# First expert table transposed by VectorE in 32x32 blocks, loaded by column quarters, in place of TensorE transposes

## The chip, the core and the metric

The kernel runs on one core of one Trainium2 chip. The metric is device time in microseconds of that core; lower is better. Five engines work beside each other, each in the order of its own queue: TensorE (PE in the rows; its weight loads are PEld), VectorE (DVE), ScalarE (ACT), GpSimd (POOL) and SyncE (SP), which here issues most of the transfers.

## What is computed

One transformer block on 512 tokens of 2048 features: an mLSTM and an S5 mixer, an output projection, and then an expert layer (PEER). The expert layer is what the change touches:

```python
def peer(x, wq, subkeys, u_tab, v_tab):
    q = (x @ wq)...                       # 512 x 2048 by 2048 x 2048
    ...                                   # top-16 of two sub-key scores, softmax gate
    def block(args):
        xt, it, gt = args
        ue = jnp.take(u_tab, it, axis=0)
        ve = jnp.take(v_tab, it, axis=0)
        act = jax.nn.gelu(jnp.einsum('td,ted->te', xt, ue))
        return jnp.einsum('te,ted->td', gt * act, ve)
```

`u_tab` (the first expert table) and `v_tab` (the second) hold 16384 experts of 2048 features in fp32, 128 MB each. `x` is the second RMS norm of the block, with the gain `norm2_g`.

## The kernel before

Of the 512 tokens, the first 128 (`NG`) take their experts by gathers (`gsteps`, L1080): for each of 128 picks of a token one indirect transfer from POOL brings 2048 features per token, and one VectorE pass of 2048 columns multiplies and sums (L1088 for the first table, L1095 for the second). The other 384 tokens (`ND`) go densely: all 16384 experts are read in 128 tiles of 128 experts, and for each tile the activations of all 384 tokens are computed.

A dense product wants the contracted dimension on the partitions. For the first table that is the feature, so a tile of 128 experts x 2048 features must be transposed. `u_load` (L1039) fetches a tile with one transfer of 1 MB, expert by partition, into `ur` (two buffers). `u_unit(i, q)` (L1049) takes a quarter, four blocks of 128 features: four TensorE transposes into one PSUM bank (L1054), then `split` (L88 to L90): ScalarE rounds the bank to `uh`, and VectorE subtracts to get the rest `ul`. `h_unit(i, q)` (L1062) is twelve matmuls of 384 columns (`mm3`, L92 to L95, three per feature block), and after the fourth quarter ScalarE applies the gelu to `hg` (L1071). `h_step` (L1103) keeps `u_unit` two quarters ahead of `h_unit`; `uh` and `ul` have four buffers each.

The order of work on every engine is that in which the Python code emits it (`manual_schedule`). What is called a unit below is one `h_step`: on VectorE the `ul` subtraction, then whatever the step pulls in from the side lists. Three stretches follow one another:

- From 1034 us: the rest of the routing of the tokens (`route_head`, `route_end`), one piece per unit.
- Then `gbuild` (L1112): for 384 tokens, four at a time, VectorE makes eight 128x128 selection matrices (L1122, L1123), TensorE multiplies four pairs, ScalarE copies the product to `Gb`. That is 96 units with such work. After each 128 tokens eight transfers issued by ScalarE write `Gb` out (L1132). In every fourth unit one gather step runs, except while these writes go out. This loop (L1140) covers 44 tiles; it ends at about 1596 us.
- From 1596 us to 3148 us the other 84 tiles (L1214). Here two units alternate with one `v_unit` (L1195) of the second table, 24 matmuls of 384 columns, from the fifth tile on. On VectorE the order of such a pair is: `ul`, `ul`, per tile a `w_stage` (L1164: product, ScalarE rounding, subtraction), one or two gather steps, the subtraction `vl` (1024 columns), two additions into `accT` (L1207).

Then the second table is finished alone (3148 to 3585 us). Ahead of all this, `load_w` (L123) loads the weights of the projections in chunks of 512 KB, 32 of them from `wq`; `norm_k` (L170) transposes the normed tokens `xs` into `xh` and `xl`, which are used by the `wq` projection and, as copies `xdh` and `xdl`, by `h_unit`.

Of the kernel before, what the change touches and what calls it, by code (L numbers as in the profile page):

```python
# [8 lines left out]
F32 = mybir.dt.float32  # L9
F32R = mybir.dt.float32r  # L10
I32 = mybir.dt.int32
U32 = mybir.dt.uint32
AF = mybir.ActivationFunctionType
OP = mybir.AluOpType
# [4 lines left out]
P = 128  # L19
T = 512  # L20
D = 2048
KB = D // P
# [8 lines left out]
def dap(ap, offset, dims):  # L31
    return bass.AP(tensor=ap.tensor, offset=ap.offset + offset, ap=dims)
# [3 lines left out]
def hybrid_block(ctx: ExitStack, tc: tile.TileContext, x, norm1_g, w_in, b_gates, conv_w, mnorm_g,  # L36
# [3 lines left out]
    v, s, g, pe, sp = nc.vector, nc.scalar, nc.gpsimd, nc.tensor, nc.sync  # L40
# [9 lines left out]

    x2 = x[0]
    win = w_in[0]
    out2 = out[0]

    consts = ctx.enter_context(tc.tile_pool(name="consts", bufs=1))
# [9 lines left out]
    def tp_bank(shape=(P, 512), dtype=F32):  # L65
        return ps.tile(list(shape), dtype, name="tp", bufs=4)
# [6 lines left out]
    with pool(name="tmp", bufs=1, side="right") as tmp:  # L73
        iota_i = tmp.tile([P, P], I32, name="iota_i")
        g.iota(iota_i, pattern=[[1, P]], base=0, channel_multiplier=-1)
        v.tensor_scalar(ident, iota_i, 0.0, None, op0=OP.is_equal)

        cst = tmp.tile([96, P], F32, name="cst")
        sp.dma_start(cst[0:64], conv_w[0].rearrange("k (c p) -> (k c) p", p=P))
        sp.dma_start(cst[64:80], norm1_g[0].rearrange("(k p) -> k p", p=P))  # L80
        sp.dma_start(cst[80:96], norm2_g[0].rearrange("(k p) -> k p", p=P))
        p = tp_bank([P, 96])
        pe.transpose(p, cst, ident[:96, :96])
        v.tensor_copy(cvec, p)
# [3 lines left out]
    def split(hi, lo, src):  # L88
        s.activation(hi, src, AF.Copy)  # L89
        v.tensor_tensor(lo, src, hi.bitcast(F32), op=OP.subtract)  # L90
# [32 lines left out]
    def load_w(src, k0, c0):  # L123
        n = NW if src is win and c0 == base["v"] else 256
        raw = wtile("wr", F32, n)
        row = src.ap[0][0]
        cut = lambda c, n: dap(src, k0 * P * row + c, [[row, P], [P * row, 4], [1, n]])
        sp.dma_start(raw[:, :, :256], cut(c0, 256))
        if n > 256:
            sp.dma_start(raw[:, :, 256:], cut(4096, 8))  # L130
        return raw
# [6 lines left out]
    OORDER = (2, 3, 0, 1)  # L138
    chunks = [(win, 4 * q, base[a] + 256 * i) for a, i in plan for q in (OORDER if (a, i) == plan[-1] else range(4))]
    chunks += [(w_out[0], 4 * q, 256 * c) for c in range(8) for q in OORDER]  # L140
    chunks += [(wq[0], 4 * q, 256 * c) for c in range(8) for q in range(4)]
    W = {"raw": [], "ready": [], "n": 0, "p": 0}

    def w_fetch():
# [25 lines left out]
    def norm_k(src, gc, k):  # L170
        p = tp_bank([P, TB, P])
        for tb in range(TB):
            pe.transpose(p[:, tb, :], src[tb][:, k * P:(k + 1) * P], ident)  # L173
        pf = p.rearrange("p b t -> p (b t)")
        s.activation(xh[:, k, :], pf, AF.Copy, scale=gc[:, k:k + 1])
        v.scalar_tensor_tensor(xl[:, k, :], pf, gc[:, k:k + 1], xh[:, k, :].bitcast(F32),
                               op0=OP.mult, op1=OP.subtract)

    XQ = {"n": 16, "f": None}

# [12 lines left out]
    for tb in range(TB):  # L193
# [3 lines left out]
        r = rstd(n1, ss, 1, 1.0 / D, "r1")  # L197
# [681 lines left out]
    with pool(name="n2", bufs=1) as n2:  # L879
        xs = [n2.tile([P, D], F32, name=f"xs{tb}") for tb in range(TB)]  # L880
        ss = n2.tile([P, TB], F32, name="ss2")
        v.tensor_reduce(ss, ssq, axis=AX.X, op=OP.add)
        r = rstd(n2, ss, TB, 1.0 / D, "r2")
        for tb in range(TB):
            if tb < 2:
                v.tensor_scalar(xs[tb], h1[:, tb, :], r[:, tb:tb + 1], None, op0=OP.mult)
            else:
                s.activation(xs[tb], h1[:, tb, :], AF.Copy, scale=r[:, tb:tb + 1])
        for k in range(KB):
            norm_k(xs, g2c, k)  # L890
        g2 = n2.tile([P, D], F32, name="g2")
        bcast_row(g2, norm2_g, D)
        for b in range(NB):
            v.tensor_tensor(xG[b], xs[b], g2, op=OP.mult)
        sk = n2.tile([P, 2, P], F32, name="sk")
        sp.dma_start(sk, subkeys[0].rearrange("a k d -> k a d"))
        p = tp_bank([P, 2, P])
        for a in range(2):
            pe.transpose(p[:, a, :], sk[:, a, :], ident)
        v.tensor_copy(subT, p)  # L900
        g.iota(iotaF, pattern=[[1, P]], base=0, channel_multiplier=0, allow_small_or_imprecise_dtypes=True)
# [136 lines left out]

    def u_load(i):  # L1039
        ur = up.tile([P, D], F32, name="ur", bufs=2)  # L1040
        sp.dma_start(ur, u2[i * P:(i + 1) * P, :])
        UT["r", i] = ur

    u_load(0)
# [2 lines left out]
    accG = [up.tile([P, D], F32, name=f"accG{i}") for i in range(NB)]  # L1047

    def u_unit(i, q):  # L1049
        ur = UT["r", i]  # L1050
        p = tp_bank([P, 4, P])
        for a in range(4):
            k = q * 4 + a
            pe.transpose(p[:, a, :], ur[:, k * P:(k + 1) * P], ident)  # L1054
        uh = up.tile([P, 4, P], F32R, name="uh", bufs=4)
        ul = up.tile([P, 4, P], F32R, name="ul", bufs=4)
        split(uh, ul, p)
        UT["u", i, q] = (uh, ul)
        if q == 3 and i + 2 < NTL:
            u_load(i + 2)  # L1060
# [282 lines left out]
```

## Time and profile before

| | us |
|---|---|
| median of 3 runs | 3587.71 (3583.08 to 3588.83) |
| span of the profiled execution | 3585.1 |
| of it: before the first unit | 1034 |
| units with routing and `gbuild` (44 tiles) | 562 |
| units beside the second table (84 tiles) | 1552 |
| second table alone, end | 437 |

The span runs from the first to the last instruction of one profiled execution; it is 2.6 us less than the median. Over the whole span TensorE is busy for 97%, VectorE for 68%, ScalarE for 34%. A group row gives busy time and mean duration of one instruction, and behind the second bar the idle time of the engine right before it and what ended that. Successive instructions of VectorE overlap a little in the rows: the next one starts before the duration of the last is over.

### The profile page before, as it was taken

What the parts mean: (1) busy time and instruction counts of PE and PEld (TensorE: products, weight loads), DVE (VectorE), ACT (ScalarE), POOL (GpSimd) and SP (SyncE); (2) the same over time, 40 slices, a digit from 0 to 9 for tenths busy, and PEclk for the clock granted to TensorE, in tenths of its full rate; (3) what the DMA queues carried; (4) which work ended last, traced back from release to release, by engine and by line L of the source; (5) the groups of instructions that cost most, each with busy time, mean ns of one, the idle gap of its engine ahead of it and who ended that gap; (6) DMA issues with size and microseconds to landing.
All of it is one profiled execution on the core that took longest, in us unless ns stands there. A gap on an engine that the chain in (4) does not pass through costs nothing.

```text
span 3585.1 us, 53549 instructions
## 1 busy us (share of the span) xinstructions
PE 3473.1 (97%) x21436; PEld 3326.9 (93%) x21436; DVE 2434.8 (68%) x4689; ACT 1208.4 (34%) x1854; POOL 464.8 (13%) x403
## 2 busy tenths in 40 slices
PE   7999999999999999999999999999999999999998
PEld 6888888997889999999999999999999999999997
DVE  7567444325998776846777777777777777766666
ACT  5344554325233333323322222222222222222333
POOL 2001110000000000002222222222222222200000
PEclk9999999999999999999999999999999999999999
DMA  4423443542324567487777767777777777664553
GB/s 143 111 80 103 110 112 105 166 132 84 95 101 159 192 218 233 167 304 269 271 283 279 275 261 268 282 282 277 267 276 274 279 281 266 261 234 169 176 178 119
DMA packets 309706, 729.86 MB, mean 204 GB/s; under 512 B 28240, under 2 KB 183888, under 8 KB 258896
## 3 DMA queue, kind: packets, MB, share of 16 engines
q1 hardware_dynamic: 215824, 411.92, 33.4%
q0 software_dynamic: 44096, 289.34, 22.0%
q10 hardware_dynamic: 49536, 25.17, 2.3%
q8 instruction: 169, 2.77, 0.3%
q14 instruction: 81, 0.66, 0.1%
HBM read 673.40 MB, written 50.59 MB: 202 GB/s over the span
## 4 chain that ended last, share of the span: by engine, by line
issue 38%; PE 35%; DMA 10%; DVE 8%; POOL 6%; ACT 2%; POOLq 0%; ACTq 0%; SPq 0%; DVEq 0%
PE mm L95 11%; PE mm L94 11%; PE mm L93 11%; DMA gr<-in_peer_v_dram,gidx 9%; POOL gr L1076 5%; DVE accG L1095 2%; DVE ul L90 1%; PE tp L1054 1%; POOL Tt L691 1%; DVE vl L90 1%; DVE wl L90 1%; DMA gr<-in_peer_u_dram,gidx 0%; PE tp L173 0%; PE tp L1003 0%; DVE accT L1207 0%
## 5 line engine op out<-in xcount | busy, mean ns | idle before, releaser
L93 PE MATMUL mm<-xdh,uh 128*128 128x384 f32 x2048 | 734.9, 359 | 12.5 <-ACT uh L89 12.5
L95 PE MATMUL mm<-ewh,vl 128*128 128x384 f32 x2048 | 692.8, 338 | 27.0 <-DVE vl L90 27.0
L95 PE MATMUL mm<-xdh,ul 128*128 128x384 f32 x2048 | 693.1, 338 | 3.1 <-DVE ul L90 1.7
L93 PE MATMUL mm<-ewh,vh 128*128 128x384 f32 x2048 | 690.8, 337 | 5.0 <-ACT vh L89 5.0
L94 PE MATMUL mm<-xdl,uh 128*128 128x384 f32 x2048 | 690.7, 337 | 0.0
L94 PE MATMUL mm<-ewl,vh 128*128 128x384 f32 x2048 | 689.6, 337 | 0.0
L89 ACT ACTIVATE uh<-tp 128x512 fp32r<-128x512 f32 x512 | 305.4, 597 | 993.5 <-PE tp L1054 948.4
L90 DVE TENSOR_TENSOR ul<-tp,uh 128x512 fp32r<-128x512 f32 x512 | 343.0, 684 | 255.5 <-ACT uh L89 255.4
L95 PEld LDWEIGHTS mm<-ewh,vl 128*128 128x128 f32 x2048 | 387.5, 189 | 34.2 <-DVE vl L90 34.0
L93 PEld LDWEIGHTS mm<-xdh,uh 128*128 128x128 f32 x2048 | 387.5, 189 | 14.4 <-ACT uh L89 14.1
L95 PEld LDWEIGHTS mm<-xdh,ul 128*128 128x128 f32 x2048 | 386.4, 189 | 7.8 <-DVE ul L90 7.8
L93 PEld LDWEIGHTS mm<-ewh,vh 128*128 128x128 f32 x2048 | 387.6, 189 | 5.3 <-ACT vh L89 5.3
L94 PEld LDWEIGHTS mm<-xdl,uh 128*128 128x128 f32 x2048 | 388.7, 190 | 0.0
L94 PEld LDWEIGHTS mm<-ewl,vh 128*128 128x128 f32 x2048 | 387.5, 189 | 0.0
L1095 DVE SCALAR_TENSOR_TENSOR accG<-gr,acts,accG 128x2048 f32<-128x2048 f32 x127 | 298.1, 2347 | 96.4 <-DMA gr<-in_peer_v_dram,gidx 95.7
L90 DVE TENSOR_TENSOR wl<-wr,wh 128x1024 fp32r<-128x1024 f32 (+1 forms) x144 | 187.1, 1302 | 249.5 <-ACT wh L89 249.4
L1088 DVE SCALAR_TENSOR_TENSOR gr<-gr,xG 128x2048 f32<-128x2048 f32 x128 | 292.1, 2286 | 79.3 <-DMA gr<-in_peer_u_dram,gidx 79.3
L90 DVE TENSOR_TENSOR vl<-vr,vh 128x1024 fp32r<-128x1024 f32 x256 | 312.5, 1221 | 43.8 <-ACT vh L89 43.7
L1076 POOL DMA_INDIRECT gr<-in_peer_u_dram,gidx x128 | 177.6, 1387 | 1262.7 <-DVE gr L1088 957.8
L1207 DVE TENSOR_TENSOR accT<-mm,accT 128x384 f32<-128x384 f32 x496 | 257.4, 549 | 84.1 <-PE mm L95 84.1
L1054 PE MATMUL tp<-ident,ur 128*128 128x128 f32 x2048 | 306.7, 272 | 0.3 <-DMA ur<-in_peer_u_dram 0.3
L93 PE MATMUL mm<-wh,xh 128*128 128x256 f32 (+1 forms) x1024 | 295.3, 288 | 0.0
(393 smaller groups left out, 5315.1 us busy)
## 6 DMA issues: line engine op xcount, KB each, us to landing
ur<-in_peer_u_dram SPq DMA_DIRECT2D x128, 1024.0 KB, 6.2
vr<-in_peer_v_dram SPq DMA_DIRECT2D x128, 1024.0 KB, 5.0
wr<-in_w_in_dram SPq DMA_DIRECT2D x80, 512.0 KB, 3.7
gt_d<-Gb ACTq DMA_DIRECT2D x24, 1024.0 KB, 12.1
gt<-gt_d SPq DMA_DIRECT2D x128, 192.0 KB, 7.6
wr<-in_w_out_dram SPq DMA_DIRECT2D x32, 512.0 KB, 3.6
wr<-in_peer_wq_dram SPq DMA_DIRECT2D x32, 512.0 KB, 3.5
hg_d<-hg SPq DMA_DIRECT2D x44, 192.0 KB, 2.6
```

Source lines behind the costliest of these rows:

```text
L89: s.activation(hi, src, AF.Copy)
L90: v.tensor_tensor(lo, src, hi.bitcast(F32), op=OP.subtract)
L93: pe.matmul(o, ah, bh, start=start, stop=False)
L94: pe.matmul(o, ah, bl, start=False, stop=False)
L95: pe.matmul(o, al, bh, start=False, stop=stop)
L691: g.dma_start(Tt[b % 2][j * 16:(j + 1) * 16, :, j:, :], Ks[:, :, 0:8 - j, :])
L1054: pe.transpose(p[:, a, :], ur[:, k * P:(k + 1) * P], ident)
L1076: g.indirect_dma_start(out=t, out_offset=None, in_=tab, in_offset=bass.IndirectOffsetOnAxis(ap=gidx[:, b, j:j + 1], axis=0))
L1088: v.scalar_tensor_tensor(t, t, 1.0, xG[b], op0=OP.mult, op1=OP.mult, accum_out=acts[:, b, j:j + 1])
L1095: v.scalar_tensor_tensor(accG[b], t, acts[:, b, j:j + 1], accG[b], op0=OP.mult, op1=OP.add)
L1207: v.tensor_tensor(a, o, a, op=OP.add)
```

## The change

Transposing moves from TensorE to VectorE, which transposes 32x32 blocks inside each group of 32 partitions. For the blocks to come out right, a tile of the first table is loaded by column quarters: partitions 32q to 32q+31 hold column quarter q of the tile, four groups of 32 experts side by side. One VectorE instruction over 128 x 512 then gives a `ut` in SBUF with 128 features on the partitions. Which features stand together changes (a block k now holds columns 32k to 32k+31 of each quarter), so the norm gain, the normed tokens and the rows of `wq` are put in the same order. `uh` and `ul` go from four buffers to three, and `ut` has two.

```diff
+    wqt = wq[0]
...
-        sp.dma_start(cst[80:96], norm2_g[0].rearrange("(k p) -> k p", p=P))
+        sp.dma_start(cst[80:96].rearrange("k (q d) -> k q d", q=4),
+                     norm2_g[0].rearrange("(q k d) -> k q d", q=4, k=KB))
...
+        if src is wqt:
+            for q in range(4):
+                sp.dma_start(raw[q * 32:q * 32 + 32],
+                             dap(src, (q * 512 + k0 * 32) * row + c0, [[row, 32], [32 * row, 4], [1, 256]]))
+            return raw
...
+    def quads(t):
+        return t.rearrange("t (k q d) -> t q k d", k=KB, q=4)
...
         for tb in range(TB):
+            o, i = quads(xs[tb]), h1[:, tb, :].rearrange("t (q k d) -> t q k d", q=4, k=KB)
             if tb < 2:
-                v.tensor_scalar(xs[tb], h1[:, tb, :], r[:, tb:tb + 1], None, op0=OP.mult)
+                v.tensor_scalar(o, i, r[:, tb:tb + 1], None, op0=OP.mult)
             else:
-                s.activation(xs[tb], h1[:, tb, :], AF.Copy, scale=r[:, tb:tb + 1])
+                s.activation(o, i, AF.Copy, scale=r[:, tb:tb + 1])
...
-            v.tensor_tensor(xG[b], xs[b], g2, op=OP.mult)
+            fv = lambda t: t.rearrange("t (q k d) -> t q k d", q=4, k=KB)
+            v.tensor_tensor(fv(xG[b]), quads(xs[b]), fv(g2), op=OP.mult)
...
     def u_load(i):
         ur = up.tile([P, D], F32, name="ur", bufs=2)
-        sp.dma_start(ur, u2[i * P:(i + 1) * P, :])
+        for q in range(4):
+            sp.dma_start(ur[q * 32:q * 32 + 32].rearrange("p (e c) -> p e c", e=4),
+                         dap(u2, i * P * D + q * 512, [[D, 32], [32 * D, 4], [1, 512]]))
...
     def u_unit(i, q):
-        ur = UT["r", i]
-        p = tp_bank([P, 4, P])
-        for a in range(4):
-            k = q * 4 + a
-            pe.transpose(p[:, a, :], ur[:, k * P:(k + 1) * P], ident)
-        uh = up.tile([P, 4, P], F32R, name="uh", bufs=4)
-        ul = up.tile([P, 4, P], F32R, name="ul", bufs=4)
-        split(uh, ul, p)
+        ut = up.tile([P, 4, P], F32, name="ut", bufs=2)
+        uh = up.tile([P, 4, P], F32R, name="uh", bufs=3)
+        ul = up.tile([P, 4, P], F32R, name="ul", bufs=3)
+        uq = UT["r", i].rearrange("p (e k d) -> p k e d", e=4, k=KB)
+        v.transpose(ut.rearrange("p k (e d) -> p k e d", e=4), uq[:, q * 4:q * 4 + 4])
+        split(uh, ul, ut)
         UT["u", i, q] = (uh, ul)
```

## Rows read from the trace of the kernel before

**Rows 1.** The page, part 1: busy time, share of span, instructions.
```profile
PE 3473.1 (97%) x21436; PEld 3326.9 (93%) x21436; DVE 2434.8 (68%) x4689; ACT 1208.4 (34%) x1854; POOL 464.8 (13%) x403
```
**Rows 2.** Costliest groups, TensorE: the transposes of the first table.
```profile
L1054 PE MATMUL tp<-ident,ur 128*128 128x128 f32 x2048 | 306.7, 272 | 0.3 <-DMA ur<-in_peer_u_dram 0.3
```
**Rows 3.** Busy time by stretch: PE, PEld, DVE, ACT, POOL; granted clock, DMA share, GB/s.
```profile
0.00:90.00 90.00, 68.32 (x305) 55.73 (x306) 63.25 (x150) 47.74 (x49) 25.65 (x43) 0.98 0.49 143
...
1034.00:1136.00 102.00, 98.11 (x603) 94.45 (x602) 92.83 (x393) 37.84 (x67) 2.95 (x3) 0.98 0.38 138
...
1596.00:3148.00 1552.00, 1526.13 (x9177) 1508.37 (x9176) 1136.48 (x1288) 443.28 (x677) 353.11 (x227) 0.99 0.73 275
```
**Rows 4.** Timeline of TensorE over one plain unit: start, duration, instruction.
```profile
1590.08 0.60 PE L1054 MATMUL tp<-ident,ur 128*128 128x128 f32 x4
...
1592.26 0.34 PE L94 MATMUL mm<-xdl,uh 128*128 128x384 f32 x1
...
1592.43 0.34 PE L95 MATMUL mm<-xdh,ul 128*128 128x384 f32 x1
...
1592.61 0.60 PE L1054 MATMUL tp<-ident,ur 128*128 128x128 f32 x4
```
**Rows 5.** Groups of VectorE from 1033.5 to 1136 us (routing): the subtractions.
```profile
L90 DVE TENSOR_TENSOR ul<-tp,uh 128x512 fp32r<-128x512 f32 x38 | 25.6, 681 | 5.8 <-ACT uh L89 5.8
```
**Rows 6.** Timeline of VectorE over one tile of gbuild.
```profile
1195.06 2.28 DVE L1088 SCALAR_TENSOR_TENSOR gr<-gr,xG 128x2048 f32<-128x2048 f32 x1
...
1197.27 0.69 DVE L90 TENSOR_TENSOR ul<-tp,uh 128x512 fp32r<-128x512 f32 x1
1197.87 0.34 DVE L1122 TENSOR_SCALAR A<-iotaF,i1T,gT 128x128 f32<-128x128 f32 x1
...
1199.69 0.68 DVE L90 TENSOR_TENSOR ul<-tp,uh 128x512 fp32r<-128x512 f32 x1
...
1208.74 2.28 DVE L1088 SCALAR_TENSOR_TENSOR gr<-gr,xG 128x2048 f32<-128x2048 f32 x1
```
**Rows 7.** Waits of VectorE, 1596 to 3148 us: total us, times, longest.
```profile
DVE ul L90 <- ACT uh L89: 116.8, 110, 2.0
DVE accG L1095 <- DMA gr<-in_peer_v_dram,gidx: 95.7, 34, 5.9
DVE gr L1088 <- DMA gr<-in_peer_u_dram,gidx: 72.4, 28, 6.0
DVE hg L1166 <- ACT hg L1071: 64.6, 53, 1.4
DVE ewl L90 <- ACT ewh L89: 48.5, 82, 0.6
```
**Rows 8.** Timeline of one w_stage: VectorE, ScalarE and VectorE in turn.
```profile
2012.66 0.56 DVE L1166 TENSOR_TENSOR hg<-hg,gt 128x384 f32<-128x384 f32 x1 [1.23 <-ACT hg L1071]
2013.25 0.53 ACT L89 ACTIVATE ewh<-hg 128x384 fp32r<-128x384 f32 x1 [0.62 <-DVE hg L1166]
...
2013.81 0.56 DVE L90 TENSOR_TENSOR ewl<-hg,ewh 128x384 fp32r<-128x384 f32 x1 [0.59 <-ACT ewh L89]
```
**Rows 9.** Groups by shape: single-input VectorE passes, ScalarE over 512 SBUF columns.
```profile
L984 DVE TENSOR_REDUCE ii<-eq 128x64 f32<-128x1024 f32 x16 | 18.7, 1209 | 0.0
L198 DVE TENSOR_SCALAR xt<-xt,r 128x2048 f32<-128x2048 f32 x4 | 5.1, 1286 | 0.1
L351 ACT ACTIVATE qT<-qT 128x512 f32<-128x512 f32 x8 | 5.1, 632 | 7.4 <-DVE qT L349 7.3
```
**Rows 10.** DMA issues: tile, engine, count, KB each, median us to landing.
```profile
ur<-in_peer_u_dram SPq DMA_DIRECT2D x128, 1024.0 KB, 6.2
vr<-in_peer_v_dram SPq DMA_DIRECT2D x128, 1024.0 KB, 5.0
wr<-in_peer_wq_dram SPq DMA_DIRECT2D x32, 512.0 KB, 3.5
```
**Rows 11.** Timeline of SyncE: issue of one tile of the first table.
```profile
1191.95 0.33 SPq L1041 DMA_DIRECT2D ur<-in_peer_u_dram  x1
```

More of the change, by code (lines that the diff above doesn't have):

```diff
@@ L140, in hybrid_block @@
     chunks += [(w_out[0], 4 * q, 256 * c) for c in range(8) for q in OORDER]
-    chunks += [(wq[0], 4 * q, 256 * c) for c in range(8) for q in range(4)]
+    chunks += [(wqt, 4 * q, 256 * c) for c in range(8) for q in range(4)]
     W = {"raw": [], "ready": [], "n": 0, "p": 0}
```

## The prediction

> **What bounds the kernel now.** The share of busy time comes first: TensorE 97%, VectorE 68% [rows 1]. That speaks for moving work from the one to the other, and the group of transposes shows what there is to move: 2048 of them, 306.7 us of busy time [rows 2]. But a share is a mean over stages, so the next view is the busy time by stretch [rows 3]. In the 102 us of routing VectorE is busy for 92.8; beside the second table for 1136 of 1552. There TensorE is busy for 1526: it bounds that stretch. Then the order inside a unit: the timeline of TensorE for what a transpose costs there, that of VectorE for what stands next to what, and the waits of VectorE for what of its idle time is really free.
>
> **What TensorE gains.** A plain unit goes from one burst of four transposes to the next in 1592.61 - 1590.08 = 2.53 us, and two neighbouring matmuls start 0.17 us apart [rows 4]. Twelve such steps (at 0.173, from several of them) are 2.08, so a burst costs 0.45 us. Over 512 units that is 230 us, if TensorE bounded every unit and nothing else came late. The next latest thing is VectorE, so the rest is a sum over VectorE's queue.
>
> **What VectorE pays in a unit.** Two things. The transpose itself, 128 x 512 in fp32, is not in the trace. The subtraction of the same 512 columns takes 0.681 [rows 5]; a single-input pass of 1024 columns takes 1.209 [rows 9], which lies on the same line (0.53 for 512 more columns). I take 0.68. From below, a pass of 2048 columns in 1.286 [rows 9] and one of 128 columns in 0.34 [rows 6] give 0.53 for 512, if the transpose ran at that better rate. From above, two passes or several smaller instructions: 1.21, the row of 1024 columns.
>
> The second is a wait that the change adds. On VectorE's queue the order is now transpose, subtraction, with ScalarE's rounding between them: VectorE cannot subtract before ScalarE has read `ut`, and everything queued behind (selection matrices, gathers, `vl`, `accT`) waits with it. Before, the rounding waited for TensorE, while VectorE did other work. That such a trip is idle time is shown by `w_stage`, which has the same shape: product, rounding, subtraction, and 0.59 us of idle for a rounding of 0.53 with 0.03 on each side [rows 8]. Over 512 columns from SBUF ScalarE takes 0.632 [rows 9], so the trip is 0.69. ScalarE is free for it: it is 34% busy [rows 1], and the buffer it writes (three now, not four) is that of a quarter whose matmuls come ahead of the last `v_unit` or unit. In all x = 0.68 + 0.69 = 1.37 us per unit (bounds 1.22 and 1.90).
>
> A rule speaks against the change. In this trace a burst costs TensorE 0.11 us per 128x128 block [rows 4]. The Trainium skill, "VectorE: DVE Perf Modes", Rules for kernel authors, says to transpose 128x128 on TensorE where a PSUM result will do; its section The three transpose paths has 390 ns for TensorE and 311 ns for VectorE's block transpose of 128x128 in bf16. The burst here is far below the first. From the second, with 384 columns more at one per cycle of its 0.96 GHz, a transpose of 512 columns would be 0.71 us, an estimate, and the forecast below 14 us longer. No run here shows that price.
>
> **The sum by stretch, against the span of 3585.1 us.**
> - Routing, 38 units [rows 5]: VectorE bounds it already, its subtractions wait for 5.8 us in all. 38 x 1.37 - 5.8 = +46.3.
> - `gbuild`, 96 units in 24 tiles: a tile takes 1208.74 - 1195.06 = 13.68 us, set by TensorE. VectorE's own work in it is a gather pass, 1197.27 - 1195.06 = 2.21, four subtractions of 1197.87 - 1197.27 = 0.60, and four times the matrices, 1199.69 - 1197.87 = 1.82 [rows 6]: 11.89. With 4 x 1.37 it is 17.37, past TensorE's 13.68 - 4 x 0.45 = 11.88. +3.69 x 24 = +88.6.
> - The other 42 units of the 44 tiles: while `Gb` is written out, ScalarE's issues set the pace, unchanged; in plain units VectorE comes to 1.37 + 0.60 + 2.21/4 = 2.52 where TensorE took 2.53. 0 (with x = 1.90, +0.52 each, +22).
> - Beside the second table, 84 tiles, 336 units: VectorE is busy for 1136.5 us and waits for the rest; five waits make 398 [rows 3, 7]. New: 1136.5 + 336 x 1.37 = 1596.8. The `w_stage` trip stays, 48.5. The old wait for `uh` is replaced. The wait for the gelu (mean 1.2) goes, since VectorE arrives 2 x 1.37 later per pair. The waits for gathers (168 us, mean 2.7, longest 6.0) mostly go for the same reason: the two trips and transposes lie between the release of a gather buffer and its next use. I keep a quarter, 45; bounds 0 and 168. That makes 1690; before 1552: +138. TensorE needs 1552 - 336 x 0.45 = 1401 and is no bound.
> - After 3148 us nothing changes: 0.
>
> Sum +273. 3585.1 + 273 = 3858; the median lies 2.6 above the span: 3861 us, 7.6% slower.
>
> **Edits costed at nothing.** Loads: per tile four issues in place of one, 3 x 0.33 us more on SyncE's queue [rows 11], which sits in tile periods of 14 to 20 us; the loads of `vr`, `gt` and `hgl` queued behind come 1 us later and are two buffers ahead. A tile lands in 6.2 us; pieces of 2 KB, as `vr` has, land in 5.0 [rows 10], so smaller pieces alone cost nothing. Cover: a load is issued a whole tile (17 to 20 us in the new schedule) ahead of its use. `wq` chunks land in 3.5 us [rows 10] in the front part; uncovered by 1 us each they would be 32 us, I take 0. The reordered norm, gain and `xG` are the same instructions over runs of 32 columns: five passes of 2048 columns, within 10 us even at double. The 0.03 us by which ScalarE is slower from SBUF lies inside the trip.
>
> **Rivals.**
> - *Faster: the trip is hidden.* If the transposes ran far enough ahead of their subtractions (or transpose and trip together were cheap), x would be 0.68. Then routing +20, `gbuild` 24 x (11.89 + 2.72 - 13.68) = +22, second-table stretch 1136.5 + 228.5 + 48.5 = 1413.5, -138: 3585.1 - 96 + 2.6 = 3492 us. It decides at x = 0.88, where 470 x = 5.8 + 43 + 367 (the three constants of the sum, without gather waits). For it: VectorE's 68%. Against: the two stand next to each other in the code, `ut` having two buffers doesn't reorder a queue, and the idle of [rows 8]. Chance 0.07; an x near 0.88, and so no change, 0.03.
> - *Transpose at two passes* (x = 1.90): routing +66, `gbuild` +139, rest +22, second-table stretch 1136.5 + 638 + 48.5 + 45 = 1868, +316; 4131 us. Chance 0.09.
> - *The quarter loads bound.* Each now fills 32 partitions. If a quarter took as long as a tile does now, a tile would take 4 x 6.2 = 24.8 us, more than the 20.1 (1690/84) of the new schedule: +531 beside the second table, 24 x 11.1 = +267 in `gbuild`, at least 4386. It decides at 17 us. Nothing in the trace shows a large transfer to 32 partitions. Chance 0.04.
> - *TensorE's clock falls.* TensorE would idle for about 290 us of 1690. If that brought it from 2.4 to 1.2 GHz for over a fifth of its work there (1401 x 1.21 = 1690), it would be the bound again; for two fifths the stretch takes 1401 x 1.4 = 1961, and the run 4132 us. Against: in the first 90 us it is busy for only 68 and is granted 0.98 [rows 3]. Chance 0.03.
> - *It doesn't do what it says*: the instruction might be issued in pieces; that is the two-pass price.
>
> **How the numbers follow.** Forecast 0.74 at 3861, its own range 3816 to 3984 (all gather waits gone, or all 168 us kept). The range must hold the bounds of the transpose: at x = 1.22, 40.6 + 74 + 43 (no gather wait) = +158, 3745; at 1.90, 4131. So 3745 to 4131; left out are the faster rival, no change, the loads and the clock, 0.17. A measurement of this kernel can tell about 0.2% from no change, 7 us. Faster 0.07, same 0.03, slower 0.90.
>
> **What would show it.** VectorE's transposes at about 0.68 us, and in front of the `ul` subtractions a wait of 0.6 to 0.7 in nearly all 512. VectorE's busy share at 74% or more with its other idle time nearly gone; TensorE below 92%, waiting for `ul`, `vl` or a selection matrix. A tile of `gbuild` at 17.4 us, a tile beside the second table at 20. The gather waits at a third or less. The prediction is wrong if the wait in front of `ul` is short, if a transpose is not near 0.68, or if VectorE waits for `ur`.

## The result and the profile after

The changed kernel takes 3872.98 us (median of 4 runs, 3871.52 to 3877.39), the kernel before 3587.0 beside it: a ratio of 1.0805 [1.079, 1.082]. The forecast was 3861, the range 3745 to 4131. The profiled execution has a span of 3869.8 us.

The page, part 1, answers to [rows 1]:

```profile
PE 3462.8 (89%) x19388; PEld 3225.9 (83%) x19388; DVE 2773.3 (72%) x5201; ACT 1213.3 (31%) x1854; POOL 498.1 (13%) x403
```

TensorE has 2048 instructions fewer and its share fell from 97% to 89%; VectorE's rose from 68% to only 72%: it has 338 us more of work in a run that is 285 us longer, and still idles for 1096 us. The groups of VectorE by shape (count, busy us, mean ns, idle time in front of them) say where:

```profile
L1068 DVE STREAM_TRANSPOSE ut<-ur 128x512 f32<-128x512 f32 x512 | 359.7, 702 | 1.3 <-PE mm L97 1.3
L92 DVE TENSOR_TENSOR ul<-ut,uh 128x512 fp32r<-128x512 f32 x512 | 354.5, 692 | 434.4 <-ACT uh L91 434.4
```

A quarter is one instruction of 702 ns. In front of the 512 subtractions that follow, VectorE is idle for 434 us, every microsecond of it ended by ScalarE's rounding: that is the wait that the change set in VectorE's way. Idle time stood there before too,

```profile
L90 DVE TENSOR_TENSOR ul<-tp,uh 128x512 fp32r<-128x512 f32 x512 | 343.0, 684 | 255.5 <-ACT uh L89 255.4
```

but then it was ScalarE waiting for TensorE's transposes (948 us in front of `uh`), while TensorE was busy for 97% of the time; now ScalarE waits for VectorE's own (1590 us).

The busy time by stretch answers to [rows 3]; the borders are where the loop over the first 44 tiles ends (1596 before, 1755 now) and where the gathers end (3148 and 3434):

```profile
1034.00:1755.00 721.00, 590.33 (x2909) 510.74 (x2909) 537.01 (x1527) 188.78 (x339) 29.20 (x31) 0.92 0.55 158
1755.00:3434.00 1679.00, 1472.31 (x7836) 1433.06 (x7835) 1355.27 (x1622) 445.06 (x677) 386.38 (x227) 0.94 0.78 254
```

The first 44 tiles take 721 us in place of 562 (+159), the stretch beside the second table 1679 in place of 1552 (+127), the rest 436 in place of 437. Inside the first, a tile of `gbuild` in VectorE's timeline, from one gather pass to the next, answers to [rows 6]:

```profile
1307.49 2.28 DVE L1100 SCALAR_TENSOR_TENSOR gr<-gr,xG 128x2048 f32<-128x2048 f32 x1
...
1309.70 0.70 DVE L1068 STREAM_TRANSPOSE ut<-ur 128x512 f32<-128x512 f32 x1
1311.16 0.69 DVE L92 TENSOR_TENSOR ul<-ut,uh 128x512 fp32r<-128x512 f32 x1 [0.76 <-ACT uh L91]
1311.77 0.34 DVE L1134 TENSOR_SCALAR A<-iotaF,i1T,gT 128x128 f32<-128x128 f32 x1
...
1325.21 2.28 DVE L1100 SCALAR_TENSOR_TENSOR gr<-gr,xG 128x2048 f32<-128x2048 f32 x1
```

1325.21 - 1307.49 = 17.72 us against 13.68 before. From the start of a transpose to that of its subtraction 1311.16 - 1309.70 = 1.46 us pass, and nothing else of VectorE's queue runs in the 0.76 of it that are idle. VectorE's waits beside the second table (total us, times, longest) answer to [rows 7]:

```profile
DVE ul L92 <- ACT uh L91: 259.5, 334, 1.1
DVE ewl L92 <- ACT ewh L91: 49.1, 83, 0.6
DVE accG L1107 <- DMA gr<-in_peer_v_dram,gidx: 7.2, 7, 1.8
DVE gr L1100 <- DMA gr<-in_peer_u_dram,gidx: 4.7, 9, 1.5
```

Busy 1355.3 plus these four, 320.5, is 1676 of 1679: VectorE's queue is the stretch. Of the gather waits of before (168 us) 12 are left, the wait for the gelu is gone, and TensorE is the one that waits:

```profile
PE mm L97 <- DVE vl L92: 194.6, 83, 4.3
```

### The profile page after: what moved, and what is told of

The parts are those of the page before. It is cut to its first block, busy times and chain, and to the rows that moved or that the text cites. A ratio compares the mean times of both kernels' runs of the same rounds, so it can differ in the third digit from the quotient of the medians.

```text
span 3869.8 us, 50857 instructions
## 1 busy us (share of the span) xinstructions
PE 3462.8 (89%) x19388; PEld 3225.9 (83%) x19388; DVE 2773.3 (72%) x5201; ACT 1213.3 (31%) x1854; POOL 498.1 (13%) x403
## 4 chain that ended last, share of the span: by engine, by line
issue 40%; PE 27%; DVE 17%; POOL 5%; DMA 5%; ACT 5%; ACTq 0%; SPq 0%; DVEq 0%; POOLq 0%
PE mm L97 9%; PE mm L96 8%; PE mm L95 8%; POOL gr L1088 4%; DVE accG L1107 3%; DVE ut L1068 3%; ACT uh L91 3%; DMA gr<-in_peer_v_dram,gidx 3%; DVE vl L92 2%; DVE accT L1219 2%; DVE ul L92 1%; POOL Tt L701 1%; DVE wl L92 1%; DMA gr<-in_peer_u_dram,gidx 1%; DVE hg L1178 0%
## 5 line engine op out<-in xcount | busy, mean ns | idle before, releaser
L97 PE MATMUL mm<-ewh,vl 128*128 128x384 f32 x2048 | 732.0, 357 | 197.0 <-DVE vl L92 196.4
L91 ACT ACTIVATE uh<-ut 128x512 fp32r<-128x512 f32 x512 | 323.3, 632 | 1678.9 <-DVE ut L1068 1590.4
L95 PE MATMUL mm<-ewh,vh 128*128 128x384 f32 x2048 | 717.5, 350 | 5.4 <-ACT vh L91 5.4
L96 PE MATMUL mm<-ewl,vh 128*128 128x384 f32 x2048 | 715.3, 349 | 0.0
L92 DVE TENSOR_TENSOR ul<-ut,uh 128x512 fp32r<-128x512 f32 x512 | 354.5, 692 | 434.4 <-ACT uh L91 434.4
L97 PEld LDWEIGHTS mm<-ewh,vl 128*128 128x128 f32 x2048 | 408.9, 200 | 232.7 <-DVE vl L92 232.1
L95 PEld LDWEIGHTS mm<-ewh,vh 128*128 128x128 f32 x2048 | 409.3, 200 | 6.0 <-ACT vh L91 6.0
L96 PEld LDWEIGHTS mm<-ewl,vh 128*128 128x128 f32 x2048 | 408.4, 199 | 0.0
L1068 DVE STREAM_TRANSPOSE ut<-ur 128x512 f32<-128x512 f32 x512 | 359.7, 702 | 1.3 <-PE mm L97 1.3
L92 DVE TENSOR_TENSOR vl<-vr,vh 128x1024 fp32r<-128x1024 f32 x256 | 312.6, 1221 | 44.0 <-ACT vh L91 44.0
L1088 POOL DMA_INDIRECT gr<-in_peer_v_dram,gidx x128 | 224.3, 1752 | 726.5 <-DVE accG L1107 675.9
```

Source lines behind the costliest of these rows:

```text
L95: pe.matmul(o, ah, bh, start=start, stop=False)
L96: pe.matmul(o, ah, bl, start=False, stop=False)
L97: pe.matmul(o, al, bh, start=False, stop=stop)
L1068: v.transpose(ut.rearrange("p k (e d) -> p k e d", e=4), uq[:, q * 4:q * 4 + 4])
L1088: g.indirect_dma_start(out=t, out_offset=None, in_=tab, in_offset=bass.IndirectOffsetOnAxis(ap=gidx[:, b, j:j + 1], axis=0))
```

## The experiments

The theory: the time is VectorE's queue, and of its new content the exposed trip to ScalarE (transpose, rounding, subtraction next to each other) costs more than the transposes. Rivals: the loads by column quarters cost the time; the three buffers do; VectorE has too little room even with the trip hidden. All ratios are to the kernel before. An edit is shown against the changed kernel, for e3_bufs3 and e10_pieces against the kernel before, and where another run is named, against that one; ... marks lines left out.

**The transposes made cheap, the trip kept** (e6_quarter: one of the four 128-column blocks of a quarter is transposed).

```diff
...
-        v.transpose(ut.rearrange("p k (e d) -> p k e d", e=4), uq[:, q * 4:q * 4 + 4])
+        v.transpose(ut[:, 0:1].rearrange("p k (e d) -> p k e d", e=4), uq[:, q * 4:q * 4 + 1])
```

> The changed kernel with a transpose of only the first of the four blocks of a quarter (128 columns in place of 512; the other three blocks of ut are zeros set once, so that part of the transposing is left out). The dependency of ScalarE on VectorE and the wait behind it stay whole. Theory: the transpose falls from 0.70 to about 0.30, the wait in front of ul stays at 0.76. Per unit 0.25 + 0.76 = 1.01: routing +33, gbuild 24 x (11.89 + 4.04 - 13.68) = +54, beside the second table 1136 + 336 x 1.02 + 49 + 60 = 1588, +36; total about 3710 us (3680 to 3740), still slower than before although hardly anything is transposed on VectorE. Rival (the pass is what costs, the trip is absorbed): about 3450 to 3500 us.

3712.72 us, 1.0356 [1.0333, 1.038]. The groups of VectorE:

```profile
L92 DVE TENSOR_TENSOR ul<-ut,uh 128x512 fp32r<-128x512 f32 x512 | 354.5, 692 | 446.6 <-ACT uh L91 446.6
L1072 DVE STREAM_TRANSPOSE ut<-ur 128x128 f32<-128x128 f32 x512 | 154.8, 302 | 0.0
```

As expected: 205 us less of transposes took 160 us off, so the transposes are a real term, and the kernel is still 3.6% slower than before with a wait as long as in the changed kernel (447 us for 434). In the rows the trip is the larger of the two terms (434 us of idle time to 360 of transposes). This run doesn't show that the wait alone would make the kernel slower: 155 us of transposes are left in it.

**The trip hidden by one unit** (e1_defer: the transpose and rounding of unit n + 2, `u_tr`, now stand ahead of the subtraction of unit n + 1, `u_sub`).

```diff
...
+            u_tr(*units[un[0]])
             un[0] += 1
+            if un[0] > 1:
+                u_sub(*units[sn[0]])
+                sn[0] += 1
...
```

> The changed kernel with one thing moved: the subtraction of a quarter is emitted one unit later, behind the transpose of the next quarter, so that ScalarE's rounding runs while VectorE transposes. Same instructions, same buffers. Theory (VectorE's queue, with the exposed trip to ScalarE as half of it): per unit 0.65 us of transpose and 0.60 of subtraction are left, the wait of 0.76 in front of the subtraction is gone. Routing 38 x 0.65 - 5.8 = +19 against the kernel before, gbuild 24 x (11.89 + 2.6 - 13.68) = +19, beside the second table VectorE 1136 + 336 x 0.65 + 49 = 1403, TensorE 1401, with some gather waits 1430: -122. Total about 3500 us (3465 to 3560), faster than both kernels. Rival (the transposing pass alone, or the loads, or fewer buffers cost the 286 us): the wait only changes its place and the time stays within 1% of 3873.

3729.59 us, 1.0404 [1.0387, 1.0421]: the wait of 434 us fell to 62 (59 of them in the first 44 tiles), but only 143 us came off the changed kernel. Waits of VectorE beside the second table:

```profile
DVE hg L1192 <- ACT hg L1088: 137.0, 83, 4.4
DVE accT L1233 <- PE mm L97: 71.2, 61, 1.5
...
DVE ul L1076 <- ACT uh L1068: 2.8, 3, 2.3
```

and of TensorE there:

```profile
PE mm L97 <- DVE ul L1076: 207.1, 113, 9.9
```

The first 44 tiles behaved as expected (they end at 1628, +32 on before, where +38 was worked out). Beside the second table the subtraction is ready one unit ahead of TensorE instead of two. As I read it, a gather pass, `vl` and two `accT` passes in front of it then leave TensorE without work, and the gelu and `accT` come late to VectorE. I had priced the hidden trip and not the shorter lead, and missed by 230 us; the next run keeps the lead. (Its expectation quotes these waits from a shorter window, 1740 to 3200 us.)

**The trip hidden, the lead kept** (e5_deep: transpose three units ahead, subtraction two; `uh` with four buffers, `hgl` with one).

```diff
-        uh = up.tile([P, 4, P], F32R, name="uh", bufs=3)
...
+        uh = up.tile([P, 4, P], F32R, name="uh", bufs=4)
...
+        while sn[0] < len(units) and sn[0] < n + 3:
+            while un[0] < len(units) and un[0] < sn[0] + 2:
+                u_tr(*units[un[0]])
+                un[0] += 1
+            u_sub(*units[sn[0]])
+            sn[0] += 1
...
-            hg = ep2.tile([P, ND], F32, name="hgl", bufs=2)
+            hg = ep2.tile([P, ND], F32, name="hgl", bufs=1)
```

> The deferred subtraction again, with one unit more of lookahead: at unit n VectorE transposes quarter n+3 and subtracts for n+2 (four buffers for uh; one instead of two for hgl makes the room). Its first form took 3730 us: the 44 tiles of routing and gbuild came out as worked out (+33 us against the kernel before, worked out +38), but beside the second table the stretch stayed at 1665 us, with VectorE waiting 113 us for the gelu and 67 for second-table products and TensorE 174 us for ul: the subtraction came one unit closer to its use. Theory (that shorter lookahead ate the gain): the stretch falls to 1440 to 1500 us, where VectorE (1404 of work) and TensorE (1401) meet; total 3490 to 3570 us. Rival (the second-table stretch is held by something else, say gathers or loads): it stays above 1600 and the total above 3680.

3643.40 us, 1.017 [1.0151, 1.019], over the expected range and under the rival's. Beside the second table the trip's wait is 0.2 us and TensorE's wait for `ul` 18 us in place of 207, so the lead did its part; but VectorE has a new wait there:

```profile
DVE hg L1189 <- DMA gt<-gt_d: 103.1, 45, 11.6
```

SyncE's timeline has the reason:

```profile
2619.38 1.96 SPq L1054 DMA_DIRECT2D ur<-in_peer_u_dram  x4
2621.38 0.45 SPq L1180 DMA_DIRECT2D gt<-gt_d  x1
2624.67 0.39 SPq L1203 DMA_DIRECT2D vr<-in_peer_v_dram  x1
```

The last transpose of a tile now comes a step earlier, so its four `ur` loads stand in front of the load of `gt`, which is due the same tile.

**That order put right** (e8_gt: e5_deep with the load of `gt` issued one step earlier).

```diff
-        if q == 1:
+        if q == 0:
             g_load(i)
         h_step(i, q)
```

> The VectorE transposition with both halves pulled apart (transposition three units ahead, subtraction two, as in e5_deep), and the load of gt now issued on SyncE one step earlier, ahead of the four quarter loads of the first table instead of behind them. Theory: the 103 us of e5_deep's second-table stretch in which the product hg = hg x gt waited for gt came only from that order on SyncE's queue, and go; some comes back as gather waits (48 us there, 168 before). Stretch 1575 -> 1480 to 1510, total about 3550 (3520 to 3590), so just under the kernel before. Rival: the loads are late because the DMA engines are full, and not for their order; then the wait only moves to gt's own load or to vr and the total stays at 3620 to 3650.

3587.60 us, 1.0004 [0.9995, 1.0014]: 56 us off, inside the expected range, and exactly level with the kernel before. The waits of VectorE beside the second table:

```profile
DVE hg L1189 <- ACT hg L1088: 51.4, 83, 2.3
DVE ewl L92 <- ACT ewh L91: 49.2, 83, 0.6
DVE accG L1112 <- DMA gr<-in_peer_v_dram,gidx: 34.4, 27, 3.8
DVE gr L1105 <- DMA gr<-in_peer_u_dram,gidx: 28.2, 21, 2.8
DVE hg L1189 <- DMA gt<-gt_d: 4.9, 1, 4.9
```

Of the 103 us 4.9 are left, which settles their cause; only 56 came off, because the waits for the gelu and for gathers grew. From the first product `hg` to the 84th this stretch takes 3145.3 - 1637.3 = 1508 us, before 3149.2 - 1606.1 = 1543; the 31 us by which it starts later are what the first 44 tiles lose. Hiding the trip and keeping the order of the loads took 285 us off the changed kernel, with every transpose still in place.

**The other exposed trip hidden too** (e9_ewl: e8_gt with the subtraction of `w_stage` behind the gathered row of its step).

```diff
-        split(wh, wl, hg)
+        s.activation(wh, hg, AF.Copy)
...
+        return lambda: v.tensor_tensor(wl, hg, wh.bitcast(F32), op=OP.subtract)
...
-            w_stage(i)
+            w_sub = w_stage(i)
...
+            if q == 3:
+                w_sub()
...
```

> e8_gt, and in the second-table stretch the subtraction for ewl is put behind the gathered rows of its step instead of directly behind its ScalarE copy (the second place in this loop where VectorE waits for its own partner, 49 us in 84 tiles). Theory: a wait on the bound engine goes, so 20 to 45 us less than e8_gt: about 3520. Rival: the gathers or vr end last there already, VectorE waits as long for them, and the total is within 10 us of e8_gt.

3525.92 us, 0.9832 [0.9814, 0.9849], 62 us below e8_gt and the best kernel of this study. Waits of VectorE:

```profile
DVE hg L1189 <- ACT hg L1088: 53.9, 83, 1.8
DVE gr L1105 <- DMA gr<-in_peer_u_dram,gidx: 33.1, 19, 4.7
DVE accG L1112 <- DMA gr<-in_peer_v_dram,gidx: 29.7, 19, 3.0
...
DVE ewl L1194 <- ACT ewh L1192: 0.6, 1, 0.6
```

49 us of wait brought 62, and no other wait of the list grew by more than 5. With both trips hidden the changed kernel is 1.7% faster than the kernel before. Not all of that is the transposition's: the kernel before has the second trip too (48.5 us, [rows 7]), and hiding it there wasn't tried. TensorE is idle for only 1552 - 1526 = 26 us of that stretch [rows 3], so it could win about that much at most there (an estimate), which leaves some 35 of the 60.

**The subtraction given to GpSimd** (e7_pool).

```diff
-        split(uh, ul, ut)
+        s.activation(uh, ut, AF.Copy)
+        g.tensor_tensor(ul, ut, uh.bitcast(F32), op=OP.subtract)
```

> The changed kernel with the subtraction moved from VectorE to GpSimd, which can do it now that ut lies in SBUF and not in PSUM. VectorE then has the transpose in place of the subtraction (0.65 for 0.60 per unit) and nothing of it waits for ScalarE. Theory: VectorE is back at the work of the kernel before, TensorE without its transposes bounds: gbuild 24 x 12.1 (-38), routing 0, beside the second table 1440 to 1480 (-72 to -112). Total 3435 to 3490 us, the best of all, if GpSimd takes under 2.5 us for 512 columns. Rival (VectorE's passes and GpSimd's get in each other's way, or gather issues come late behind the subtractions): VectorE's two-input passes lengthen or gather waits grow past 250 us, 3600 or more.

3921.76 us, 1.0938 [1.0919, 1.0956], slower than the change itself; the rival came true. GpSimd's group:

```profile
L1070 POOL TENSOR_TENSOR ul<-ut,uh 128x512 fp32r<-128x512 f32 x512 | 833.8, 1643 | 1325.3 <-ACT uh L1069 1293.2 <-PE mm L97 16.2 <-PE tp L1141 10.5
```

VectorE's groups and, below them, its waits beside the second table:

```profile
L92 DVE TENSOR_TENSOR vl<-vr,vh 128x1024 fp32r<-128x1024 f32 x256 | 351.3, 1372 | 44.0 <-ACT vh L91 43.9
L1135 DVE TENSOR_SCALAR A<-iotaF,i1T,gT 128x128 f32<-128x128 f32 x384 | 217.5, 566 | 0.0
```

```profile
DVE accG L1108 <- DMA gr<-in_peer_v_dram,gidx: 227.6, 58, 8.9
DVE gr L1101 <- DMA gr<-in_peer_u_dram,gidx: 156.9, 44, 8.6
```

Two things went wrong at once. GpSimd also issues the gathers, and they queue behind a subtraction that waits for ScalarE: 384 us of gather waits. And some of VectorE's own passes stood still beside GpSimd's (`A` 566 ns on average against 341 in the changed kernel, `vl` 1372 against 1221):

```profile
1312.59 1.38 DVE L1135 TENSOR_SCALAR A<-iotaF,i1T,gT 128x128 f32<-128x128 f32 x1
...
1312.59 1.29 POOL L1070 TENSOR_TENSOR ul<-ut,uh 128x512 fp32r<-128x512 f32 x1 [3.47 <-ACT uh L1069]
```

The averages hide two kinds of `A`: 96 of the 384 take 1.30 us, each beside a subtraction of GpSimd, the others 0.32. So it is with `vl` (36 of 256 take 2.30 us, the others 1.22), but not with the transposes (0.72 at most) or `accT` (0.56 at most). The trip wasn't removed; it was moved to a queue with worse things behind it.

**No transposition at all** (e4_none: the rows go untransposed into rounding and subtraction).

```diff
-        ut = up.tile([P, 4, P], F32, name="ut", bufs=2)
...
-        v.transpose(ut.rearrange("p k (e d) -> p k e d", e=4), uq[:, q * 4:q * 4 + 4])
-        split(uh, ul, ut)
+        uq = UT["r", i].rearrange("p (k d) -> p k d", k=KB)
+        split(uh, ul, uq[:, q * 4:q * 4 + 4])
```

> The changed kernel without any transposition of the first table: rounding and subtraction read the loaded tile itself (so the dense activations are of untransposed data). Leaves out the transpose and the dependency of ScalarE on VectorE. Theory: VectorE gets back 1.4 us per unit and TensorE, without its transposes, bounds: routing 96 us (-5), gbuild 24 x 11.9 (-43), beside the second table 1401 to 1430 (-122 to -151). Total 3385 to 3420 us: the most that taking the transposes off TensorE can give. Rival (VectorE or the gathers bound below that): above 3450.

3451.32 us, 0.9624 [0.9604, 0.9643], over the theory's range and just inside the rival's. So taking the whole transposition off TensorE, with the quarter loads of the change kept, gives 136 us, not the 230 of the prediction's first step. From the changed kernel to e8_gt to this one, hiding the trip brings 285 us and leaving out the transposes another 136; in another order the shares differ, as e6_quarter shows (160 with the trip in place). Beside the second table TensorE is busy for 1391 of 1452 us and waits for `vl`, and VectorE in front of that for its gathers and the gelu:

```profile
DVE accG L1105 <- DMA gr<-in_peer_v_dram,gidx: 95.7, 53, 3.9
DVE hg L1176 <- ACT hg L1081: 71.4, 59, 2.2
DVE gr L1098 <- DMA gr<-in_peer_u_dram,gidx: 64.7, 39, 3.9
...
PE mm L97 <- DVE vl L92: 51.5, 31, 3.2
```

**The buffers alone** (e3_bufs3: the kernel before with three buffers for `uh` and `ul`).

```diff
-        uh = up.tile([P, 4, P], F32R, name="uh", bufs=4)
-        ul = up.tile([P, 4, P], F32R, name="ul", bufs=4)
+        uh = up.tile([P, 4, P], F32R, name="uh", bufs=3)
+        ul = up.tile([P, 4, P], F32R, name="ul", bufs=3)
```

> The kernel before with three buffers for uh and ul in place of four, nothing else. Theory: the buffers don't matter, because a quarter is rounded only after its four transposes, which stand behind the matmuls that free the third buffer: 3587 us, within 7. Rival (fewer buffers take slack): slower by 10 to 60 us, with ScalarE waiting for matmuls before uh.

3584.33 us, 0.9996 [0.9986, 1.0005]: nothing.

**The loads alone** (e2_loads: the quarter loads and the reordered columns of the change, transposed by TensorE as before, with four buffers).

```diff
-        ut = up.tile([P, 4, P], F32, name="ut", bufs=2)
...
-        v.transpose(ut.rearrange("p k (e d) -> p k e d", e=4), uq[:, q * 4:q * 4 + 4])
-        split(uh, ul, ut)
...
+        for a in range(4):
+            k = q * 4 + a
+            pe.transpose(p[:, a, :], ur[:, k * P:(k + 1) * P], ident)
...
+        split(uh, ul, p)
```

> Only the data movement of the change: quarter loads of the first table and of wq, reordered gain, normed tokens and xG; the first table is transposed by TensorE as before, with four buffers. The dense activations are then taken over mismatched features, which is left so: it has no bearing on time. Theory: the loads are covered and the reordered passes cost nothing: 3587 us, within 15. Rival (the quarter loads to 32 partitions or the reordered front cost part of the 286 us): 3620 or more, with waits of TensorE for ur or of ScalarE for wr.

3610.81 us, 1.006 [1.0037, 1.0082], between the theory and its rival: the loads cost some 22 us where I had put nothing. Busy time beside the second table:

```profile
1596.00:3174.00 1578.00, 1540.42 (x9175) 1522.07 (x9174) 1138.23 (x1288) 442.79 (x676) 349.99 (x227) 0.98 0.83 270
```

The DMA share is 0.83 where before had 0.73 [rows 3], for the same bytes. `vr` lands after 6.6 us in place of 5.0, the gathered rows of the first table after 8.4 in place of 7.1. Of the 26 us by which this stretch is longer, TensorE's waits for `vl` and `ur` are 11 (37.2 for 25.9) and its busy time 14 (1540 for 1526, at a granted clock of 0.98 for 0.99); how the loads lead to the second part isn't shown.

**Small pieces, full width** (e10_pieces: the kernel before, each tile loaded in four transfers of 2 KB a row to all 128 partitions).

```diff
-        sp.dma_start(ur, u2[i * P:(i + 1) * P, :])
+        for q in range(4):
+            sp.dma_start(ur[:, q * 512:q * 512 + 512], u2[i * P:(i + 1) * P, q * 512:q * 512 + 512])
```

> The kernel before, with each first-table tile loaded as four transfers of column quarters (2 KB of each row) to all 128 partitions; nothing else changed. e2_loads, whose quarter loads also went to 32 partitions each and in four pieces per partition, cost 22 to 26 us. Theory A, the size of the pieces is what costs (2 KB in place of 8 KB): the DMA share of the second-table stretch rises from 0.73 to about 0.83 and the total is 3605 to 3615. Theory B, the narrow destination of 32 partitions is what costs: share and time stay at those of the kernel before, 3580 to 3592.

3566.83 us, 0.9949 [0.9931, 0.9966], below both theories' ranges: the pieces cost nothing, and the kernel even gains 0.5% (its gather waits up to 3129 us are 133 us against 166; why they fall wasn't tried). Against this kernel e9_ewl is ahead by 41 us. What SyncE's queue took of the 16 DMA engines (packets, MB, share of the span) in the kernel before,

```profile
q1 hardware_dynamic: 215824, 411.92, 33.4%
```

in e10_pieces,

```profile
q1 hardware_dynamic: 271120, 411.95, 34.9%
```

and in e2_loads:

```profile
q1 hardware_dynamic: 272704, 411.95, 39.0%
```

Times the spans that is 1197, 1244 and 1408 us: almost the same packets cost 47 us more than before when they fill 128 partitions and 211 when they fill 32. (In e2_loads the loads of `wq` are narrow too, 17 MB of the 412.) So the narrow destination is what costs, as in theory B, though its share and time weren't quite those of before: the DMA share of the second-table stretch is 0.77, between 0.73 and 0.83. The Trainium skill, "SBUF — State Buffer", section "Can I just issue two DMAs to hit both halves?", says that the ports are picked by the partition span of a single transfer, so that only one over all 128 reaches all of them; the two runs agree, though no view shows ports.

**The same tile in full-width loads** (e11_rowcut: e9_ewl with the loads cut by 32 rows; each fills 512 columns of all partitions).

```diff
-        for q in range(4):
-            sp.dma_start(ur[q * 32:q * 32 + 32].rearrange("p (e c) -> p e c", e=4),
-                         dap(u2, i * P * D + q * 512, [[D, 32], [32 * D, 4], [1, 512]]))
+        for e in range(4):
+            sp.dma_start(ur[:, e * 512:e * 512 + 512],
+                         dap(u2, (i * P + e * 32) * D, [[512, 4], [D, 32], [1, 512]]))
```

> e9_ewl, with each first-table tile cut into its four loads another way: by blocks of 32 rows, each load going to all 128 partitions (2 KB to each), instead of by column quarters, each going to 32 partitions (4 pieces of 2 KB to each). What stands in ur afterwards is the same. Theory: the 22 to 26 us of e2_loads came from the narrow destination (e10_pieces, 2 KB pieces on 128 partitions, cost nothing and was 18 us faster than the kernel before), so the DMA share of the second-table stretch falls from 0.90 to about 0.85, the gather waits (63 us) shrink and the total is 15 to 40 us below e9_ewl's 3526: 3485 to 3511. Rival: there the loads are no longer what ends last, VectorE is (1325 of 1451 us busy), and the total stays within 10 us of e9_ewl.

4005.30 us, 1.1171 [1.1156, 1.1186]: both my theory and its rival were far off. SyncE's queue took 31.6% of 4005.3, 1266 us, against 40.8% of 3529.4, 1440, in e9_ewl, so the DMA engines did spend less time; but the loads came late. VectorE's waits from 1700 to 3560 us:

```profile
DVE ut L1067 <- DMA ur<-in_peer_u_dram: 243.2, 47, 11.2
...
DVE ut L1067 <- issue: 76.3, 16, 7.5
```

and SyncE's timeline, where the four issues took 2.3 us in e9_ewl:

```profile
2304.64 5.86 SPq L1054 DMA_DIRECT2D ur<-in_peer_u_dram  x4
2310.60 6.01 SPq L1206 DMA_DIRECT2D vr<-in_peer_v_dram  x1
...
2319.98 11.30 SPq L1054 DMA_DIRECT2D ur<-in_peer_u_dram  x4
```

My reading is that the queue takes the work no faster than it drains. The new source has an outermost dimension of 4. The Trainium skill, "DMA: Bandwidth & Descriptors", section "Why a DMA increments its semaphore by 16 and not by 1", has a transfer split over as many of the 16 engines as divide the slowest dimension of both sides: by that, four here. The stalled issues fit it, and so do the semaphore increments that the trace holds: 503 of these 512 loads have five, the last of them 14.5 us after the issue (median), where 475 of e9_ewl's have sixteen, the last after 5.9. What the fifth is no view shows, none counts engines, and a cut with 32 rows outermost wasn't tried; so the cause is supported and not proved.

**The product moved too** (e12_hg: e11_rowcut with `hg` times `gt` behind the gathered row, its subtraction behind the next `vl`).

```diff
-        if q == 3:
-            w_sub = w_stage(i)
...
             if q == 3:
-                w_sub()
+                w_sub = w_stage(i)
...
+            if q == 3:
+                w_sub()
```

> e11_rowcut, with the rest of the step w_stage moved too: the product hg x gt, which in e9_ewl waits 54 us in 84 tiles for ScalarE's Gelu of the unit just computed, now comes behind the gathered row of its step, and the ewl subtraction behind the next vl. Theory: VectorE is the bound there, so the 54 us of waits go and 25 to 50 us come off e11_rowcut: 3445 to 3480. Rival: the gathers' or PE's own wait ends last in their place and less than 15 us come off.

3999.82 us, 1.1157 [1.1141, 1.1172], 5.5 us below e11_rowcut, a difference that the two intervals don't separate: less than the rival's 15 us, not the theory's 25 to 50. Of VectorE's waits from 1700 to 3560 us this one is new, and its timeline shows what it is:

```profile
DVE vl L92 <- ACT vh L91: 123.5, 81, 1.5
```

```profile
2305.77 0.55 DVE L1189 TENSOR_TENSOR hg<-hg,gt 128x384 f32<-128x384 f32 x1
...
2306.35 0.53 ACT L1192 ACTIVATE ewh<-hg 128x384 fp32r<-128x384 f32 x1 [2.16 <-DVE hg L1189]
...
2306.78 1.04 ACT L91 ACTIVATE vh<-vr 128x1024 fp32r<-128x1024 f32 x1
...
2307.86 1.22 DVE L92 TENSOR_TENSOR vl<-vr,vh 128x1024 fp32r<-128x1024 f32 x1 [1.54 <-ACT vh L91]
```

The wait for the gelu fell from 52 us to 0.6 and those for `ur` in front of the transposes from 243 to 99. In their place came longer gather waits (271 us for 148) and these 123.5: the edit itself laid a new exposed trip, product, two roundings on ScalarE's queue, `vl`. So the run doesn't show what the move alone is worth, here or in e9_ewl.

## Why the prediction was right, step by step

The sign, the mechanism and nearly the size held: 3861 forecast, 3873 measured. That it came out so near is in part luck (two errors below nearly cancel); that it came out slower is not, because the sum went by VectorE's queue and not by the share of busy time. By its terms:

- *The transpose*, taken at 0.68 between 0.53 and 1.21: 0.702, one instruction. The price by the Trainium skill, "VectorE: DVE Perf Modes", The three transpose paths (0.71 for 512 columns, an estimate), came nearer than my row of two-input subtractions.
- *The trip*, taken at 0.69: mostly 0.76 to 0.78 in the rows. x is 1.46 in `gbuild` and (1355.3 - 1136.5 + 259.5) / 336 = 1.42 beside the second table, where I had 1.37. The shape of `w_stage` [rows 8] was the right row; its rounding is over fewer columns, and I corrected that by 0.10 where 0.17 to 0.19 was due.
- *Routing*: +57 (its end, the first selection matrix, moved from 1134.3 to 1191.3) for +46.3. With x = 1.46 the same step gives +49.7. Of the 7 us left, 2 are a later start (VectorE's work ahead of the first unit ends at 1031.8 for 1029.9) and 1.7 a longer gather wait (8.7 for 7.0); the rest stays unexplained.
- *`gbuild`*: 17.72 us for 17.37 in the tile shown. 11.89 + 4 x 1.46 is 17.73: the step holds, x was small by 0.09.
- *The other 42 units*, taken at 0: 159 - 57 - 24 x 4.04 = +5, if all tiles of `gbuild` are like that one.
- *Beside the second table*: 1679 for 1690, by two errors that nearly cancel. Trip and transposes took 478 us for 460, the gathers 12 for the 45 that I kept of 168. A quarter kept was a choice without a row; nearly all went.
- *Edits costed at nothing*: here a step failed. "Smaller pieces alone cost nothing" is right (e10_pieces), but the row of `vr` [rows 10] is of pieces over 128 partitions, and the 32-partition destination costs some 22 us beside a TensorE-bound loop. In the changed kernel it hides: VectorE waits 1.3 us in front of the transposes and none of that for a load, and `vr`, at 6.7 us to landing, delays nothing in VectorE's waits. So the rival was far too dear at 4386 and "nothing" too cheap; the buffers cost nothing, as said.
- *The clock rival*: the granted clock did fall, from 0.99 to 0.92 and 0.94 in the two stretches in which TensorE idles most, and the matmuls of `ewh` and `vh` took 350 ns for 337. A mean of 0.94 between the levels 1.0 and 0.5 is 12% of the stretch at the lower one (an estimate), under the fifth at which the rival decides. It cost no time that shows, because VectorE was the bound: the fall came, the price that the rival put on it didn't.
- *The faster rival*, 3492 with the trip hidden: e8_gt is nearly that kernel, and takes 3588. Its stretch is 35 us shorter than before, not 138: the rival let the waits for the gelu (51) and for gathers (63) vanish, and they come back as soon as VectorE is early again. The prediction's own argument for their vanishing was that VectorE arrives late; the rival used it where it no longer held.
- *The 230 us that TensorE would gain* were called a gain only if nothing else came late; e4_none gives 136.
- *The signs*: the wait in front of `ul`, the single instruction near 0.68, `gbuild`, the tile of 20 us and the gather waits came as listed. VectorE's share, put at 74% or more, is 72%; that was an error of working, for the forecast's own terms give (2434.8 + 512 x 0.68) / 3858 = 72%.

## What to carry to other kernels

Work moved to an engine with a free share can be worth less than nothing if it comes as the first half of a trip to another engine and back: read whether the second half stands directly behind it on the in-order queue, and put other work between the two, without shortening the lead that the consumer needs. When steps are pulled ahead, look at what each of them issues: a load that moves up a queue pushes another back (103 us here). Price a load by a row with the same number of partitions and the same outermost dimension, not with the same bytes.

## What the hardware showed that I had not expected

- Beside a subtraction of GpSimd (1.29 us) a pass of VectorE can stand still for all of it: `A` took 1.38 us in the lines of e7_pool, 0.34 in the changed kernel. Which pass is hit goes by where the subtraction starts: 96 of 384 `A`, but only 3 of 384 `B`, which keeps its average (282 ns for 280). Transposes and `accT` took no longer beside it.
- Loads of the same 256 KB in the same 2 KB pieces differ by their shape alone: 47 us of DMA time more than whole rows on 128 partitions, 211 on 32, and with an outermost source dimension of 4 the last semaphore increment comes 14.5 us after the issue for 5.9, and four issues take up to 11 us for 2.3.
- A 128 x 512 transposition in fp32 takes VectorE 702 ns, of 128 x 128 302 ns: 1.04 ns for a column more.
- The granted clock of TensorE (1.0 is its 2.4 GHz) averaged 0.92 and 0.94 in the stretches in which it waits for VectorE, after 0.99 in the same stretches before, with waits of a few microseconds only (the longest are 7.1, for `uh`, in the first and 4.3, for `vl`, in the second).
